# Attention merge: the third output tile's first nine products move ahead of the last division

## The chip, the core and the metric

The kernel runs on one core of one Trainium2 chip. The metric is the device time of one execution in microseconds (us), first instruction to last and the little that lies around them. Five engines work side by side, each in the order of its own instruction stream: TensorE (PE) multiplies matrices, VectorE (DVE) and ScalarE (ACT) work element by element, GpSimd (POOL) does small work, and SyncE (SP) starts most transfers. Products land in PSUM, which has eight banks; everything else is in SBUF.

## The reference, cut to what matters

One layer of a transformer trunk: two token mixers on the same input, merged by gates, then a feed-forward block.

```
mla_l = _blocked_attend(q_l, k_all, v_all).reshape(B, L, -1) @ w_mla_o
y_l = (jax.nn.sigmoid(gr_l) * ret_l + jax.nn.sigmoid(gm_l) * mla_l) @ w_out
```

There are 512 latent and 256 context tokens, eight attention heads of 64 values each and 1024 model features. The change touches the product with `w_mla_o` in the first line, and the merge by the gates in the second.

## The kernel before

**Numbers in two parts.** Every matrix product is made of three: each operand is split into a rounded part and the rest (`split`, L104: ACT casts the high part, L105, DVE subtracts for the low part, L106), and `mm3` (L119) multiplies high by high (L121), high by low (L122) and low by high (L123). A weight is loaded on SP's queue into one of three raw buffers (`wr`, L109) and split into one of three pair buffers (`w`, L115).

**The heads.** Heads 0 to 7 run one after the other. `mix(h)` (L624) makes six score tiles `st` by 128 keys, exponentiates them on ACT (`ex`, L642), splits them (`pt`) and multiplies them with the values into `po` (L654 to L656). Row 64 of `po` is the softmax sum: ACT copies it to `sums` (L658) and the rest to `ou` (L659). Between these stand pieces of the next heads: `row_max(h + 1)` (products `sc`, L612, a maximum on DVE, L614, a transpose `mr` and a copy into the query, L620), `queries(h + 2)` (`mq`, L597 to L602) and `keys` (`kn`, `knc`, `kl`, `kc`).

**The division.** Two heads make a pair, whose `ou` is divided by its sums and split into `om`. The first three pairs do it through DRAM (`reciprocals`, L681: `sums` is written out, read back spread over the partitions as `sm`, inverted by DVE, L687, written as `recd`, L688, and read back broadcast as `rb`, L691; `divided`, L694, multiplies by it, L695). The last pair does it in place with TensorE (`divide`, L661): four transposes into PSUM tile `s1` (L664), the reciprocal (L666), four transposes into `s2` (L670), a split `rr`, two products that spread it over the partitions into `s3` (L674, L675), the multiplication (L676) and the split into `om`.

**The merge.** `merge_mm(n, ks)` (L800) makes output tile `n` of 128 features in PSUM tile `mo`, from those of the four pairs that `ks` names, three products for each pair. One weight tile, of `w_mo[n // 2]`, serves two output tiles. Nine products of tile 0 stand inside the last head, nine of tile 1 behind it, then the division, and then the rest of the 96. Each finished tile is multiplied with one gate, added to the other branch and split into `mg` (L821 to L823), which the output projection `wo` reads.

**What sets the order.** The program names the order in which steps are asked for; a scheduler then places every instruction on its engine and gives each tile the buffer that comes free, so a step that moves can change the order of others far ahead of it. PSUM tiles `st`, `mq`, `kn`, `mr`, `mo`, `s1`, `s2` and `s3` share four banks (`pss`, L78). `sc` and `po` share four more (`psb`, L77).

Of the kernel before, what the change touches and what calls it, by code (L numbers as in the profile page):

```python
# [63 lines left out]
def block(ctx: ExitStack, tc: tile.TileContext, xc, xtok, crow, wada, bada, w_rg, w_rv, w_rqk, w_kv, w_dq,  # L64
# [27 lines left out]
    def half(shape, dt=F32, n="hp"):  # L92
        return hpp.tile(shape, dt, tag="hp", name=nm(n))
# [4 lines left out]
    def bank(n="ps"):  # L98
        return pss.tile([P, 512], F32, tag="ps", name=nm(n))
# [4 lines left out]
    def split(h, l, src):  # L104
        S.copy(h, src)  # L105
        V.tensor_tensor(l, src, h.bitcast(F32), ALU.subtract)  # L106
# [6 lines left out]
    def weight(ap, n=1024):  # L113
        r = load(ap, n)
        w = whl.tile([P, 2, 1024], F32R, tag="w", name=nm("w"))  # L115
        split(w[:, 0, :n], w[:, 1, :n], r[:, :n])
        return w

    def mm3(o, st, mv, start, stop, more=False):  # L119

        T.matmul(o, st[0], mv[0], start=start, stop=False, skip_group_check=more)  # L121
        T.matmul(o, st[0], mv[1], start=False, stop=False, skip_group_check=more)  # L122
        T.matmul(o, st[1], mv[0], start=False, stop=stop, skip_group_check=more)  # L123
# [161 lines left out]
    def feat(w, base=0, step=P, ktn=KT):  # L285
        def st(k):
            c = slice(base + k * step, base + k * step + P)
            return w[:, 0, c], w[:, 1, c]
        return st
# [235 lines left out]
    def run(g):  # L525
        for _ in g:
            pass
# [272 lines left out]
    def merge_mm(n, ks):  # L800
        if n % 2 == 0 and wm[n] is None:
            wm[n] = wm[n + 1] = weight(w_mo[n // 2])
        if mp[n] is None:
            mp[n] = bank("mo")
        st = feat(wm[n], (n % 2) * 512)
        for k in ks:
            mm3(mp[n], st(k), (om[k][:, 0], om[k][:, 1]), k == 0, k == 3)
# [3 lines left out]
        next(m)  # L811
    merge_mm(0, range(3))
    run(m)
    merge_mm(1, range(3))
    next(eg)
    om.append(divide(ou))
    mg = [eight([P, 2, NL], F32R, "mg") for _ in range(8)]
    for n in range(8):
        merge_mm(n, range(3, 4) if n < 2 else range(4))
        m = half([P, NL], n="mt")  # L820
        V.tensor_tensor(m, mp[n], gm[n // 2][:, n % 2], ALU.mult)  # L821
        V.tensor_tensor(m, m, gr[n // 2][:, n % 2], ALU.add)
        split(mg[n][:, 0], mg[n][:, 1], m)  # L823
# [513 lines left out]
```

## Time and profile before

| what | value |
|---|---|
| median of three runs | 975.82 us (974.88 to 976.2) |
| the profiled execution | 976.76 us |
| its span, first to last instruction | 975.0 us |
| around the span | 1.76 us |
| TensorE busy | 948.1 us of the span |
| mean granted TensorE clock | 0.995 |

The profile is of one execution, 0.94 us longer than the median of the runs. A row of the timeline has a start (us from the span's start), a duration, the engine, the source line, the operation, what it writes and reads, and in brackets how long the engine had been idle and what released it.

### The profile page before, as it was taken

The numbers are of one execution on the slowest core, as the hardware profiler recorded it, in microseconds if no ns is written. First come the engines' busy times: TensorE is split into PE (matmuls) and PEld (weight loads), VectorE is DVE, ScalarE is ACT, GpSimd is POOL, SyncE is SP. The second block draws the span as 40 slices with busy tenths as digits, with TensorE's granted clock in tenths as the row PEclk, the third lists the DMA queues.
The fourth block names the chain that finished last, engine by engine and source line by source line (L and its number), as shares of the span: only waits on it lengthen the run. The fifth ranks groups of instructions, "written<-read, shape, count | busy, mean of one in ns | idle before, by whom it ended". The sixth has DMA issues, their size and how long they took to land.

```text
span 975.0 us, 13864 instructions
## 1 busy us (share of the span) xinstructions
PE 948.1 (97%) x5354; PEld 806.8 (83%) x5354; DVE 703.1 (72%) x1117; ACT 451.4 (46%) x684; POOL 67.4 (7%) x91
## 2 busy tenths in 40 slices
PE   5999999999999999999998999999999999999996
PEld 3888888888899878877675777999999999988885
DVE  6949977676773554488887778697777666794957
ACT  3354263335233633257677455265555455653340
POOL 0000100100001101000000001122122110000100
PEclk9999999999999999999999999999999999999999
DMA  9845621441115369221002368579777762676671
GB/s 354 336 141 197 240 92 45 171 152 49 30 61 175 128 157 202 87 65 44 13 12 55 108 208 251 179 193 218 189 202 176 188 155 66 219 250 188 207 235 67
DMA packets 54734, 148.84 MB, mean 153 GB/s; under 512 B 9862, under 2 KB 11014, under 8 KB 54668
## 3 DMA queue, kind: packets, MB, share of 16 engines
q1 hardware_dynamic: 41580, 123.94, 39.2%
q0 software_dynamic: 6112, 11.54, 7.1%
q10 hardware_dynamic: 6976, 12.48, 4.1%
q8 instruction: 42, 0.69, 0.3%
q14 instruction: 24, 0.20, 0.1%
HBM read 142.13 MB, written 4.23 MB: 150 GB/s over the span
## 4 chain that ended last, share of the span: by engine, by line
PE 83%; DVE 7%; ACT 4%; issue 2%; DMA 2%; POOL 1%; DVEq 0%; SPq 0%; ACTq 0%; POOLq 0%
PE wd L122 4%; PE wd L123 4%; PE wd L121 4%; PE gy L121 3%; PE gt L121 3%; PE gt L123 3%; PE gt L122 3%; PE gy L122 3%; PE gy L123 3%; PE rva L123 2%; PE rva L121 2%; PE ro L123 2%; PE ro L122 2%; PE ro L121 2%; PE rva L122 2%
## 5 line engine op out<-in xcount | busy, mean ns | idle before, releaser
L105 ACT CAST w<-wr 128x1024 fp32r<-128x1024 f32 (+2 forms) x137 | 141.3, 1032 | 193.7 <-PE wd L123 47.6
L106 DVE TENSOR_TENSOR w<-wr,w 128x1024 fp32r<-128x1024 f32 (+2 forms) x137 | 164.3, 1200 | 70.7 <-ACT w L105 69.2
L121 PE MATMUL wd<-w,tt 128*128 128x512 f32 (+1 forms) x163 | 61.2, 375 | 0.0
L122 PE MATMUL wd<-w,tt 128*128 128x512 f32 (+1 forms) x163 | 60.9, 374 | 0.1
L123 PE MATMUL wd<-w,tt 128*128 128x512 f32 (+1 forms) x163 | 60.7, 373 | 0.0
L121 PE MATMUL gt<-hL,w 128*128 128x512 f32 x128 | 50.9, 398 | 0.2 <-DVE ck L483 0.2
L123 PE MATMUL gt<-hL,w 128*128 128x512 f32 x128 | 50.7, 396 | 0.0
L122 PE MATMUL gt<-hL,w 128*128 128x512 f32 x128 | 50.7, 396 | 0.0
L405 POOL TENSOR_TENSOR sm<-sm,mhalf 128x1 f32<-128x1 f32 x18 | 15.1, 840 | 452.2 <-DVE sm L404 452.1
L122 PEld LDWEIGHTS wd<-w,tt 128*128 128x128 f32 x163 | 30.6, 188 | 6.3 <-DVE w L106 0.4
L123 PEld LDWEIGHTS wd<-w,tt 128*128 128x128 f32 x163 | 30.7, 188 | 6.1
L121 PEld LDWEIGHTS wd<-w,tt 128*128 128x128 f32 x163 | 30.6, 188 | 5.8
L106 DVE TENSOR_TENSOR pt<-ex,pt 128x512 fp32r<-128x512 f32 x48 | 30.7, 685 | 6.1 <-ACT pt L105 5.9
L510 ACT ACTIVATE gate<-gt 128x512 f32<-128x512 f32 x16 | 9.6, 598 | 50.1 <-PE gt L123 50.1
L614 DVE TENSOR_REDUCE sm<-sc 128x1 f32<-128x768 f32 x32 | 29.6, 950 | 0.8 <-PE sc L613 0.6
L121 PEld LDWEIGHTS gt<-hL,w 128*128 128x128 f32 x128 | 24.1, 188 | 6.0 <-DVE ck L483 0.5
L123 PEld LDWEIGHTS gt<-hL,w 128*128 128x128 f32 x128 | 24.1, 188 | 5.8
L122 PEld LDWEIGHTS gt<-hL,w 128*128 128x128 f32 x128 | 24.1, 188 | 5.5
L105 ACT CAST w<-s 128x1024 fp32r<-128x1024 f32 x19 | 20.0, 1050 | 18.6 <-PE gx L123 18.6
L642 ACT ACTIVATE ex<-st 128x512 f32<-128x512 f32 x48 | 26.8, 596 | 3.6 <-PE st L123 3.5
L105 ACT CAST ap<-af 128x512 fp32r<-128x512 f32 x24 | 14.8, 621 | 27.3 <-DVE af L372 25.7
L106 DVE TENSOR_TENSOR w<-s,w 128x1024 fp32r<-128x1024 f32 x19 | 23.3, 1225 | 5.6 <-ACT w L105 5.4
(441 smaller groups left out, 3100.6 us busy)
## 6 DMA issues: line engine op xcount, KB each, us to landing
wr<-in_w_dn_dram SPq DMA_DIRECT2D x44, 512.0 KB, 4.3
wr<-in_w_gu_dram SPq DMA_DIRECT2D x25, 512.0 KB, 4.2
ada_m<-in_wada_dram SPq DMA_DIRECT2D x22, 512.0 KB, 5.3
s<-in_w_gu_dram SPq DMA_DIRECT2D x38, 256.0 KB, 4.6
s<-in_w_gu_dram POOLq DMA_DIRECT2D x38, 256.0 KB, 6.6
wr<-in_w_out_dram SPq DMA_DIRECT2D x16, 512.0 KB, 4.4
wr<-in_wada_dram SPq DMA_DIRECT2D x10, 512.0 KB, 3.7
wgb<-in_w_gu_dram SPq DMA_DIRECT2D x19, 256.0 KB, 4.7
```

Of the source, the lines that this page charges most:

```text
L105: S.copy(h, src)
L106: V.tensor_tensor(l, src, h.bitcast(F32), ALU.subtract)
L121: T.matmul(o, st[0], mv[0], start=start, stop=False, skip_group_check=more)
L122: T.matmul(o, st[0], mv[1], start=False, stop=False, skip_group_check=more)
L123: T.matmul(o, st[1], mv[0], start=False, stop=stop, skip_group_check=more)
L405: G.tensor_tensor(dst, dst, mhalf[:, :n], ALU.pow)
L510: S.activation(dst[n // 2][:, n % 2], ps, AF.Sigmoid)
L614: V.tensor_reduce(mx[:, t:t + 1], ps.rearrange("p a b -> p (a b)")[:, :NA], AX.X, ALU.max)
L642: S.activation(ex, ps, AF.Exp, scale=SSC)
```

## The change

Nine of the twelve products of output tile 2 (the three pairs that are divided already) are asked for ahead of the division, as those of tile 1 are; behind it, tile 2 has three products left instead of twelve. The number of products is the same.

```diff
     merge_mm(0, range(3))
     run(m)
-    merge_mm(1, range(3))
+    for n in range(1, 3):
+        merge_mm(n, range(3))
     next(eg)
     om.append(divide(ou))
     mg = [eight([P, 2, NL], F32R, "mg") for _ in range(8)]
     for n in range(8):
-        merge_mm(n, range(3, 4) if n < 2 else range(4))
+        merge_mm(n, range(3, 4) if n < 3 else range(4))
```

`next(eg)` loads and splits one weight of the feed-forward block (`in_w_gu_dram`, `wgh` and `wgl`). With the change the weight of tiles 2 and 3 (`w_mo[1]`) is asked for ahead of it.

TensorE's order at the last division, before the change. The tiles `mo794`, `mo795`, `mo817` are output tiles 0, 1 and 2, `om804` is the last pair's quotient, and the brackets name the engines that an instruction waits for:

```order
L670 MATMUL s2801_4656<-ident_92,sm800_4654 2x128 [waits DVE_49]
L670 MATMUL s2801_4656<-ident_92,sm800_4654 2x128 x3
L674 MATMUL s3803_4664<-rr802_4661,sel_3364 128x512 [waits Activation_49]
L675 MATMUL s3803_4664<-rr802_4661,sel_3364 128x512 [waits DVE_49]
L121 MATMUL mo817_4700<-om645_4016,w816_4697 128x512 [waits PE_49]
L122 MATMUL mo817_4700<-om645_4016,w816_4697 128x512
L123 MATMUL mo817_4700<-om645_4016,w816_4697 128x512
L121 MATMUL mo817_4700<-om710_4288,w816_4697 128x512
L122 MATMUL mo817_4700<-om710_4288,w816_4697 128x512
L123 MATMUL mo817_4700<-om710_4288,w816_4697 128x512
L121 MATMUL mo817_4700<-om770_4521,w816_4697 128x512
L121 MATMUL mo794_4615<-om804_4668,w793_4612 128x512 [waits Activation_49]
```

The same place with the change, where `mo798` is output tile 2, `mo819` tile 3 and `om807` the last pair's quotient:

```order
L123 MATMUL mo798_4648<-om770_4521,w797_4645 128x512
L664 MATMUL s1802_4664<-ident_92,sums505_3362 128x64 [waits Activation_49,Pool_49]
L664 MATMUL s1802_4664<-ident_92,sums505_3362 128x64 x3
L670 MATMUL s2804_4671<-ident_92,sm803_4669 2x128 [waits DVE_49]
L670 MATMUL s2804_4671<-ident_92,sm803_4669 2x128 x3
L674 MATMUL s3806_4679<-rr805_4676,sel_3364 128x512 [waits DVE_49]
L675 MATMUL s3806_4679<-rr805_4676,sel_3364 128x512
L121 MATMUL mo819_4718<-om645_4016,w797_4645 128x512 [waits DVE_49]
L122 MATMUL mo819_4718<-om645_4016,w797_4645 128x512
L123 MATMUL mo819_4718<-om645_4016,w797_4645 128x512
L121 MATMUL mo794_4615<-om807_4683,w793_4612 128x512 [waits Activation_49]
L121 MATMUL mo795_4633<-om807_4683,w793_4612 128x512
```

The nine products of tile 2 have moved from behind the division to ahead of it; three of tile 3 stand where they stood. With three `mo` tiles held, `s1`, `s2`, `s3` and tile 3 take the one bank that is left in turn (bank 6; before, `s1` and `s3` had bank 5, `s2` and tile 2 bank 6), so L674 now waits for DVE instead of ACT, and the first product behind the division waits for DVE.

VectorE's order at the start of head 4, some 50 us ahead of the division, as a difference. `w_4645` is `w_mo[1]`, `mq_4128` and `qf_4123` are the query of head 5, `sm_4158` its row maxima, and L687 is the reciprocal of the second pair:

```order
 L597 TENSOR_TENSOR qf_4123<-mq_4113,qtab_3344 128x512
 L599 TENSOR_TENSOR q_4125<-mq_4113,qtabs_3346 32x512
+L106 TENSOR_TENSOR w_4645<-wr_4643,w_4645 128x1024
 L600 TENSOR_TENSOR qf_4123<-qf_4123,q_4125 32x512
 L106 TENSOR_TENSOR mq_4128<-qf_4123,mq_4128 128x512
 L614 TENSOR_REDUCE sm_4158<-sc_4159 128x1
 L614 TENSOR_REDUCE sm_4158<-sc_4163 128x1
+L687 RECIPROCAL sm_4150<-sm_4150 128x8
 L614 TENSOR_REDUCE sm_4158<-sc_4167 128x1
-L687 RECIPROCAL sm_4150<-sm_4150 128x8
 L614 TENSOR_REDUCE sm_4158<-sc_4171 128x1
```

The split of `w_mo[1]` has come here from a place just ahead of the division (its cast on ACT likewise, to the last place before L620 of head 4). Later in the same head the division of the second pair, L695, has moved from behind L599 of head 6's query to a place three tiles earlier, and TensorE's `sc`, `po` and `mq` products of heads 4 to 6 stand in other orders, with none added.

SP's order of transfers at the same place, as a difference; `sumd`, `sm`, `recd` and `rb` are the second pair's way through DRAM:

```order
 L691 DMA rb_3882<-recd 64x512 x2
 L684 DMA sumd<-sums_3362 1x512 x2
+L110 DMA wr_4658<-in_w_gu_dram 128x1024
 L686 DMA sm_4150<-sumd 128x2x4
 L688 DMA recd<-sm_4150 128x2x4
```

A load of 512 KB that stood ahead of the first pair's way (where `w_mo[1]` is loaded now) stands inside the second pair's.

## Rows read from the trace of the kernel before

**Rows 1.** The page: busy time of each engine, share of the span, instructions

```profile
PE 948.1 (97%) x5354; PEld 806.8 (83%) x5354; DVE 703.1 (72%) x1117; ACT 451.4 (46%) x684; POOL 67.4 (7%) x91
```

**Rows 2.** Waits of TensorE from 400 to 570 us (total, times, longest)

```profile
PE st L121 <- ACT ex L642: 1.8, 1, 1.8
```

**Rows 3.** Timeline of all engines around the last division

```profile
540.31 0.40 PE L656 MATMUL po<-pt,mv 128*65 128x512 f32 x1
...
540.74 0.58 ACT L658 COPY sums<-po 1x512 f32<-1x512 f32 x1 [1.22 <-PE po L656]
...
542.40 0.39 PE L123 MATMUL mo<-om,w 128*128 128x512 f32 x1
...
542.73 0.46 PE L664 MATMUL s<-ident,sums 64*128 64x64 f32 x4
...
544.75 0.49 PE L674 MATMUL s<-rr,sel 2*128 2x512 f32 x1 [0.66 <-ACT rr L105]
...
545.46 0.69 PE L675 MATMUL s<-rr,sel 2*128 2x512 f32 x1 [0.22 <-DVE rr L106]
...
546.08 0.80 PE L121 MATMUL mo<-om,w 128*128 128x512 f32 x1
546.19 0.69 DVE L676 TENSOR_TENSOR ou<-s,ou 128x512 f32<-128x512 f32 x1 [0.78 <-PE s L675]
...
546.67 0.63 PE L122 MATMUL mo<-om,w 128*128 128x512 f32 x1
...
546.97 0.62 ACT L105 CAST om<-ou 128x512 fp32r<-128x512 f32 x1 [2.27 <-DVE ou L676]
...
547.62 0.69 DVE L106 TENSOR_TENSOR om<-ou,om 128x512 fp32r<-128x512 f32 x1 [0.74 <-ACT om L105]
...
548.38 0.63 PE L123 MATMUL mo<-om,w 128*128 128x512 f32 x1
```

**Rows 4.** Windows: stretch, length, busy times, granted clock (PEclk), DMA share, GB/s

```profile
531.20:535.40 4.20, 4.18 (x11) 2.69 (x12) 2.51 (x4) 4.20 (x9) 0.00 (x0) 0.59 0.41 125
546.10:549.50 3.40, 3.40 (x10) 2.75 (x10) 1.39 (x2) 0.62 (x1) 0.00 (x0) 0.57 0.41 135
```

**Rows 5.** The page's groups: the low parts of weights on VectorE

```profile
L106 DVE TENSOR_TENSOR w<-wr,w 128x1024 fp32r<-128x1024 f32 (+2 forms) x137 | 164.3, 1200 | 70.7 <-ACT w L105 69.2
```

**Rows 6.** Timeline of all engines, start of head 4

```profile
486.05 0.58 ACT L620 ACTIVATE mq<-mr 1x512 fp32r<-1x512 f32 x1 [3.67 <-PE mr L618]
...
486.66 0.68 DVE L600 TENSOR_TENSOR qf<-qf,q 32x512 f32<-32x512 f32 x1
...
487.26 0.24 SPq L684 DMA_DIRECT2D sumd<-sums  x1
...
488.36 0.61 ACT L105 CAST mq<-qf 128x512 fp32r<-128x512 f32 x1
...
488.44 0.38 SPq L686 DMA_DIRECT2D sm<-sumd  x1
...
489.02 0.50 PE L612 MATMUL sc<-kl,mq 128*128 128x512 f32 x1
...
489.73 2.69 DVE L614 TENSOR_REDUCE sm<-sc 128x1 f32<-128x768 f32 x3
...
495.34 1.56 SPq L691 DMA_DIRECT2D rb<-recd  x2
```

**Rows 7.** Timeline of SyncE's queue, the first pair's way through DRAM

```profile
458.45 0.35 SPq L110 DMA_DIRECT2D wr<-in_w_gu_dram  x1
459.01 0.24 SPq L684 DMA_DIRECT2D sumd<-sums  x1
462.26 0.38 SPq L686 DMA_DIRECT2D sm<-sumd  x1
```

**Rows 8.** Timeline of VectorE, the second pair's division

```profile
502.67 0.69 DVE L695 TENSOR_TENSOR ou<-ou,rb 128x512 f32<-128x512 f32 x1
```

**Rows 9.** The view of tile `rb`: its reads' time to landing

```profile
DMA to landing us min/median/max: 2.8/3.6/3.6
```

## The prediction

> **What bounds the kernel now.** I read the page first: TensorE is busy for 948.1 of the span's 975.0 us [rows 1], so nearly every microsecond in which it waits longer or shorter comes out at the end, and no other engine is near its limit. The list of its waits has 1.8 us once, for ACT's exponentials at the end of head 6 [rows 2], and little else around the change. The timeline of the division [rows 3] is the place to look closely. The last `po` product starts at 540.31; ACT has copied the sums by 540.74 + 0.58 = 541.32. TensorE comes to the transposes L664 only at 542.73, because nine products of tile 1 stand ahead of them: from 540.31 to 542.40 nine steps of 0.232 us each. So the division doesn't wait for the sums; it waits for TensorE's own queue, by 1.4 us. After L664 come 3.35 us, to 546.08, in which TensorE has transposes and two short products and nothing else. From 546.08 it works again, on tile 2, while L676 (546.19), the cast (546.97 + 0.62 = 547.59) and the low part (547.62 + 0.69 = 548.31) finish the quotient `om`. Those 2.2 us between 546.08 and 548.31 cost nothing today, since tile 2's products lie beside them.
>
> The windows view adds one thing: TensorE's granted clock is 0.57 of full speed in 546.10 to 549.50, and 0.59 in 531.20 to 535.40 [rows 4], both times just after it had little to do. At the lower level (1.2 GHz) a product takes (548.38 - 546.67) / 4 = 0.428 us [rows 3] against 0.232 at 2.4 GHz.
>
> **The change part by part.** *The nine products of tile 2 ahead of the division.* They run at 0.232 us each, so L664 starts 2.1 us later. TensorE is busy for all of it, so this costs nothing by itself; but it fills a gap that wasn't there (the sums were ready), and takes the cover from one that was.
>
> *The division itself.* In the order shown L674 waits for DVE instead of ACT, since `s3` lies in the bank of `s2` and must wait until both parts of `rr` are read. Today that read is over at 545.46, where L675 starts, 2.73 after L664 [rows 3]. So L674 starts at 2.73 instead of 2.02, and L675 one product later, 0.23 or 0.43 by the clock: 2.96 to 3.16. From L675's start to L676's start are 0.73, and L676 takes 0.69, so its end lies 4.38 to 4.58 after L664. Tile 3's first product waits for that, as it gets the same bank: some 0.07 later, 4.5. Today the first product behind the division starts at 3.35. TensorE loses **1.15 us** here. After that nothing more is lost: the high part of `om` comes 0.78 to 1.4 us after L676's end by the same rows, and three products of tile 3, then three high ones of tiles 0 to 2, cover that at either clock (0.7 and 1.4 us at full speed).
>
> The Trainium skill (Perfetto Trace Analysis, Optimization Strategy) reads gaps on the engine that should be saturated as a sign that SBUF or PSUM may be too small for the next tile. No row of the division before has that cause. By that rule the bank that is short would be the reason of the whole loss, and giving `s3` a bank of its own would give back the 0.71 at L674 and most of the wait for L676.
>
> *The end of the merge.* DVE then gets three finished tiles at once and, in its order, splits the second `w_out` weight only after tile 7's multiplication. Counted from TensorE's first `wo` product that is about 3.3 us (a multiplication and two additions of 0.6 to 0.7, a split of 1.2 [rows 3, 5]), and the second weight's low part is wanted after 12 products and one, 3.0 us. I put down **0.15** (bounds 0 and 0.4).
>
> *The split of `w_mo[1]` in head 4.* On ACT it is free: 3.67 us idle ahead of L620 [rows 6]. On DVE 1.2 us [rows 5] now stand ahead of L600, so head 5's query is ready at 488.5 instead of 487.34; its cast, behind one more exponential in ACT's order, starts near 489.6 instead of 488.36 [rows 6]. The score products follow at 490.3, where TensorE's new order has them after two more `st` tiles, so they don't wait; but the third waits for the first maximum: low part of the query 0.7, maximum 2.69 / 3 = 0.9, so 491.85, and TensorE is through with the second near 491.0. That is **0.85 us** of idle time where there was 0.1 or less. What else moves in head 4 I cost at nothing, since other products stand ready.
>
> *The load inside the second pair's way.* SP issues the 512 KB once that split is done, about 487.95, ahead of L686. Without a load ahead L686 follows L684 after 488.44 - 487.26 = 1.18 us [rows 6]; with one 0.56 us ahead, in the first pair, after 462.26 - 459.01 = 3.25 [rows 7]. So a small transfer lands about 2.1 us later behind a load. If the read of `sm` takes as long as that write, it is there near 488.44 + 3.3 = 491.7. L687 stands behind the second maximum in the new order, at 491.85 + 0.9 = 492.75, so the read is in time, but L687 comes 0.3 later than today (behind the third, 489.73 + 2.69 = 492.42 [rows 6]). The two `rb` reads (today 495.34, and the second 1.0 later [rows 6]) move by as much and need up to 3.6 us to land [rows 9]: 496.65 + 3.6 = 500.3. L695, which today runs at 502.67 without a wait [rows 8], now stands where DVE arrives near 499.4. DVE waits almost 1 us, head 6's query is that much later, and its first score product, placed three products earlier, finds it missing: **0.65 us**. The third pair's reciprocal is also later (behind the last maximum), which delays the last `pt` of head 6 and a `po` product: **0.5**. Against this the row maxima of heads 5 and 6 stand earlier, which gives back part of the waits ahead of the next heads: **-0.5**. Together heads 4 to 6: 0.85 + 0.65 + 0.5 - 0.5 = **1.5 us**; bounds 0 (all hidden) and 2.5 (nothing given back, and 0.5 more for reads that land late).
>
> *The clock.* I assume that the two slow stretches stay as they are. One costs (0.428 - 0.232) for each of its seven or so products, 1.4 us; it can go, or a further one can come.
>
> **The sum.** 1.15 + 0.15 + 1.5 = 2.8 us. On the profiled execution that is 976.76 + 2.8 = 979.6; that one lies 0.94 above the median of the runs, so in their terms 975.82 + 2.8 = **978.6 us**, slower by 0.29%. A measurement of this kernel can tell about 0.2%, 1.95 us, from no change: 977.77 is the border.
>
> **The rivals.** *The heads hide their part, and only the division costs* (not slower in what can be measured). For it: the 1.5 is laid out from places in an order and not from rows of such waits, and TensorE has other products around each of them. Against it: TensorE works through its stream in order, and a product that waits holds those behind it. Then 975.82 + 1.3 = 977.1; it decides from the point where heads 4 to 6 cost under 0.65. Chance 0.22.
>
> *One slow stretch fewer.* The stall of 1.8 us ahead of 531.2 and the division both shift; if the clock isn't lowered after one of them, 1.4 comes back. With the heads at nothing: 977.1 - 1.4 = 975.7, no change; 0.10. With both stretches gone 974.3, or less by what the runs scatter; I give 0.05 to faster.
>
> *One slow stretch more.* TensorE idles about 1.2 us longer inside the division and works on slowly behind it, and it has new idle time in heads 4 to 6. A further stretch adds 1.4: 980.0; 0.13. By the Trainium skill (TensorE: Matmul & The Clock Gate, HAM oscillation) gaps between bursts of products lower the clock again and again; the rows agree in so far as both lowered stretches follow gaps [rows 2 to 4].
>
> **How the numbers follow.** The forecast, both parts at work, has 0.50 and a range of its own of 977.8 to 979.8. Slower by over 0.2%: 0.50 + 0.13 = 0.63. Within 0.2%: 0.22 + 0.10 = 0.32. Faster: 0.05. The range leaves out the cases of fewer slow stretches (0.15) below, and some 0.04 above: 976.2 to 980.8.
>
> **What would show it.** In the profile after: L674 released by DVE; from L664 to the first `mo` product behind it 4.5 us instead of 3.35; that product released by DVE L676; a new wait of `sc` for L614 in head 4, and DVE waiting at L695 for `rb`. The start of head 7's scores would show the 1.5, the first `wo` product the whole. It is wrong if products hide the heads' waits, if L674 starts as early as before, or if the clock's stretches are other in number.

## The result: 985.63 us, slower by 0.9%, more than three times the forecast loss

| what | before | after |
|---|---|---|
| median of four runs each | 975.46 us | 985.63 us (982.74 to 986.28) |
| ratio, 95% interval | | 1.0093 [1.0076, 1.0111] |
| profiled execution / its span | 976.76 / 975.0 us | 986.28 / 984.5 us |
| mean granted clock | 0.995 | 0.993 |

The sign was right and the size was not: 978.6 was forecast, 980.8 was the upper end. TensorE has as many instructions as before [rows 1] and waits longer; its busy time is 3.2 us longer too, part of it at the lower clock (below):

```profile
PE 951.3 (97%) x5354; PEld 808.2 (82%) x5354; DVE 703.0 (71%) x1117; ACT 452.1 (46%) x684; POOL 67.5 (7%) x91
```

Its waits from 400 to 600 us after the change (total, times, longest); the first row is the one of before [rows 2]:

```profile
PE st L121 <- ACT ex L642: 1.8, 1, 1.8
PE s L674 <- DVE rr L106: 1.4, 1, 1.4
PE po L656 <- DVE pt L106: 1.2, 1, 1.2
PE wo L122 <- DVE w L106: 1.1, 2, 0.5
PE wo L121 <- ACT w L105: 0.9, 2, 0.8
PE st L121 <- ACT mq L620: 0.9, 2, 0.7
PE mo L121 <- DVE ou L676: 0.8, 1, 0.8
PE sc L612 <- DVE sm L614: 0.8, 1, 0.8
```

The second and seventh rows are the division that the prediction described; the third and eighth are the heads. The fourth and fifth are in a place where it expected 0.15 us: the output projection (`wo`), more than 30 us behind the division. The list counts four of them, 2.0 us. By the steps from one `wo` product to the next there are five (0.57, 0.92, 1.15, 0.93 and 0.52 us between 585.0 and 594.4, where 0.23 is usual), 2.9 us more than usual.

The division, in the timeline of all engines after (answers to [rows 3]):

```profile
544.48 0.40 PE L656 MATMUL po<-pt,mv 128*65 128x512 f32 x1
...
549.00 0.46 PE L664 MATMUL s<-ident,sums 64*128 64x64 f32 x4
...
551.74 0.49 PE L674 MATMUL s<-rr,sel 2*128 2x512 f32 x1 [1.38 <-DVE rr L106]
...
552.50 0.69 DVE L676 TENSOR_TENSOR ou<-s,ou 128x512 f32<-128x512 f32 x1 [0.82 <-PE s L675]
...
553.25 0.51 PE L121 MATMUL mo<-om,w 128*128 128x512 f32 x1 [0.78 <-DVE ou L676]
```

L674 waits for DVE, and from L664 to the first product behind it are 553.25 - 549.00 = 4.25 us where 4.5 was forecast and 3.35 stood before. But L676 starts 552.50 - 549.00 = 3.50 after L664, and before 546.19 - 542.73 = 3.46 [rows 3]: for VectorE, on whose result everything behind waits, the division isn't longer. It is later, since L664 starts 4.52 us behind the last `po` instead of 2.42.

What that does, together with VectorE's new order, is seen on SyncE's queue. Loads in the output projection, before and after (a load goes out when one of the three raw buffers `wr` is free):

```profile
560.13 0.33 SPq L110 DMA_DIRECT2D wr<-in_w_out_dram  x1
563.02 0.33 SPq L110 DMA_DIRECT2D wr<-in_w_gu_dram  x1
568.24 0.33 SPq L110 DMA_DIRECT2D wr<-in_w_out_dram  x1
571.03 0.33 SPq L110 DMA_DIRECT2D wr<-in_w_gu_dram  x1
572.77 0.33 SPq L110 DMA_DIRECT2D wr<-in_w_out_dram  x1
```

```profile
569.31 0.33 SPq L110 DMA_DIRECT2D wr<-in_w_out_dram  x1
574.30 0.33 SPq L110 DMA_DIRECT2D wr<-in_w_gu_dram  x1
576.64 0.33 SPq L110 DMA_DIRECT2D wr<-in_w_out_dram  x1
577.73 0.33 SPq L110 DMA_DIRECT2D wr<-in_w_gu_dram  x1
580.08 0.33 SPq L110 DMA_DIRECT2D wr<-in_w_out_dram  x1
```

The same loads, of `w_out[3]`, a `w_gu`, `w_out[4]`, a `w_gu` and `w_out[5]`, go out 9.2, 11.3, 8.4, 6.7 and 7.3 us later, while the first `wo` product is only 571.00 - 565.66 = 5.34 us later. Each goes out just when VectorE is through with the low part of the third weight before it. Those low parts of `w_out[0]` to `w_out[3]` began before at 558.84, 561.77, 566.99 and 569.78; after (timeline of VectorE):

```profile
568.02 1.22 DVE L106 TENSOR_TENSOR w<-wr,w 128x1024 fp32r<-128x1024 f32 x1
...
573.01 1.22 DVE L106 TENSOR_TENSOR w<-wr,w 128x1024 fp32r<-128x1024 f32 x1
...
575.35 2.35 DVE L106 TENSOR_TENSOR w<-wr,w 128x1024 fp32r<-128x1024 f32 x2
```

568.02 + 1.22 = 569.24, and the load of `w_out[3]` goes out at 569.31; 573.01 + 1.22 = 574.23, and the `w_gu` load at 574.30.

**Where the 9.5 us between the two profiled executions lie.** From the starts of the same products in both timelines: 0.6 at the last `po` of head 3 (486.08 to 486.69), ahead of everything that the change moves; 3.6 from there to the last `po` of head 7 (54.23 to 57.79), of which 1.1 is a longer stretch at the lower clock (below); 1.2 from there to the first `wo` (25.35 to 26.52); 3.2 from the first to the 97th `wo`, the first half of the projection (22.92 to 26.09); 1.0 from there to the end, which no run here follows up.

### The profile page after: what moved, and what is told of

Same layout as the page of the kernel before. It is cut to its first block, busy times and chain, and to the rows that moved or that the text cites. A ratio compares the mean times of both kernels' runs of the same rounds, so it can differ in the third digit from the quotient of the medians.

```text
span 984.5 us, 13862 instructions
## 1 busy us (share of the span) xinstructions
PE 951.3 (97%) x5354; PEld 808.2 (82%) x5354; DVE 703.0 (71%) x1117; ACT 452.1 (46%) x684; POOL 67.5 (7%) x91
## 4 chain that ended last, share of the span: by engine, by line
PE 83%; DVE 6%; ACT 4%; DMA 4%; issue 2%; POOL 1%; SPq 0%; DVEq 0%; ACTq 0%; POOLq 0%
PE wd L122 4%; PE wd L123 4%; PE wd L121 4%; PE gy L121 3%; PE gy L122 3%; PE gy L123 3%; PE gt L121 3%; PE gt L123 3%; PE gt L122 3%; PE rva L121 2%; PE rva L123 2%; PE ro L123 2%; PE ro L121 2%; PE ro L122 2%; PE rva L122 2%
## 5 line engine op out<-in xcount | busy, mean ns | idle before, releaser
L105 ACT CAST pt<-ex 128x512 fp32r<-128x512 f32 x48 | 27.3, 623 | 0.2
```

## The experiments

Runs of one kernel differ by up to 6.4 us, in part with the number and length of TensorE's stretches at the lower clock (the mean granted clock of single runs lies between 0.992 and 0.999), so each time is given with its interval beside the kernel before on the same chip. In most runs the order of some instructions is *held*: an edge between each and the next sets the order in which an engine's queue takes them, and no more.

```
for a, b in zip(ins, ins[1:]):
    tc.add_manual_dep(b.ins, a.ins.name, info, reason="row")   # info: NoSync
```

The table counts, in the timeline of TensorE of each profiled execution, us from the last `po` of head 7 to the first, the 97th and the last of the 192 `wo` products (*late clock*: whether the stretch behind the division ran partly at half the clock, which costs 1.5 to 2.7 ahead of the first `wo`).

| run | first `wo` | 97th | first to 97th | last | late clock | ratio [95%] |
|---|---|---|---|---|---|---|
| before | 25.35 | 48.27 | 22.92 | 73.14 | yes | |
| after | 26.52 | 52.61 | 26.09 | 77.64 | yes | 1.0093 [1.0076, 1.0111] |
| e1 hoist only | 25.40 | 48.22 | 22.82 | 73.48 | yes | 1.0035 [1.0019, 1.0051] |
| e2 products only | 26.50 | 52.47 | 25.97 | 78.79 | yes | 1.0050 [1.0031, 1.0069] |
| e3 + VectorE held | 26.51 | 53.88 | 27.37 | 78.09 | yes | 1.0048 [1.0030, 1.0065] |
| e4 order only | 23.85 | 48.88 | 25.03 | 73.96 | no | 1.0032 [1.0017, 1.0046] |
| e5 + ScalarE held | 26.47 | 51.53 | 25.06 | 75.75 | yes | 1.0042 [1.0028, 1.0057] |
| e6 change, both held | 26.53 | 51.22 | 24.69 | 75.43 | yes | 1.0086 [1.0063, 1.0109] |
| e7 division first | 23.83 | 46.36 | 22.53 | 74.49 | no | 1.0039 [1.0025, 1.0054] |
| e8 `s3` own bank | 23.84 | 49.25 | 25.41 | 74.04 | no | 1.0031 [1.0018, 1.0043] |
| e9 own buffers | 27.58 | 49.97 | 22.39 | 73.91 | yes | 0.9997 [0.9985, 1.0010] |
| e10 before, own buffers | 23.85 | 46.24 | 22.39 | 70.18 | no | 0.9984 [0.9973, 0.9995] |
| e11 change, own buffers | 27.72 | 50.12 | 22.40 | 74.04 | yes | 1.0044 [1.0029, 1.0059] |
| e12 division earlier, own buffers | 22.74 | 45.13 | 22.39 | 70.75 | no | 0.9962 [0.9947, 0.9977] |
| e13 hoist, third pair | 25.43 | 50.30 | 24.87 | 74.46 | yes | 1.0016 [1.0002, 1.0029] |
| e14 division earlier | 22.71 | 46.57 | 23.86 | 73.33 | no | 0.9995 [0.9981, 1.0008] |

**The first four: which part costs what.** e1 asks for the weight early and moves no product; e2 moves the products without asking earlier:

```diff
 e1, in the kernel before            e2, in the kernel after
+    wm[2] = wm[3] = weight(w_mo[1])  -    for n in range(1, 3):
     next(eg)                         -        merge_mm(n, range(3))
     om.append(divide(ou))            +    merge_mm(1, range(3))
                                           next(eg)
                                      +    merge_mm(2, range(3))
```

In e1 heads 4 to 6 and SyncE's order are those of the changed kernel, and VectorE's order in the merge that of before; in e2 it is the reverse. e3 is e2 with VectorE's merge held in the order of before; e4 is the kernel before with it held in the order of after (its casts on ScalarE then fall as in the changed kernel too).

> The kernel before, with the weights w_mo[1] asked for ahead of the next(eg) but the nine products of tile 2 left behind the division. Heads 4 to 6 and SyncE's transfers then stand in the order of the changed kernel, the merge behind the division in that of the kernel before. If the 9.8 us fall into three parts that add up (heads 4 to 6 about 2.5 to 3.3 with the longer slow stretch behind them, division about 1, output projection about 3), this one costs 2.5 to 3.5 us: 978 to 979.5. If instead the early load of w_mo[1] is what makes the loads of w_out late, the waits of the output projection are here too: 981 to 983.

> The change with the next(eg) ahead of tile 2's products instead of behind them: nine products in front of the division, heads 4 to 6 and SyncE's order as in the kernel before, VectorE's order in the merge as in the changed kernel. If the parts add up: division 1 and output projection 3, 979 to 981, with first waits of wo for w in the output projection. If the late loads come from the heads: 976.5 to 977.5, and no such waits.

> As the run with the products alone, and VectorE's instructions in the merge held in the order of the kernel before (m0 m1 a0 a1 m2 g0 g1 a2 m3, w_mo[3], g2 a3 m4, w_out[0], g3 a4 m5, w_out[1], ...) by edges that only set an order; TensorE's order then differs from the kernel before by the nine products alone. If VectorE's order is the cause of the late loads, only the division is left: about 1 us, 976.5 to 977.5, without waits of wo for w. If the moved products themselves make the loads late (the merge begins later but ends as fast), the time stays at 979 to 981.

> The kernel before with nothing changed but VectorE's order in the merge, which is held in that of the changed kernel (m4 m5 g3 a4 a5, w_out[0], g4 g5 m6 m7 a6 a7, w_out[1], g6 g7, w_out[2], w_out[3]); TensorE's and SyncE's orders are those of the kernel before. If VectorE's order makes the loads of w_out and w_gu late, this alone costs 2.5 to 3.5 us: 978 to 979.5, with waits of wo for w from the sixth w_out on, and the first w_gu load issued 8 us or more later than before. If the order costs only what it delays directly (as the prediction had it, 0 to 0.4): 975.5 to 976.5.

Measured: e1 979.94, e2 982.88, e3 980.92, e4 978.80 us, beside 975.70. Heads and merge nearly add up (0.35% and 0.50% for 0.93% together), and the late loads are not the heads' doing: e1 has one wait of `wo` of 0.5 us, e2 has 2.4 us of them. VectorE's order alone (with the casts that follow it) costs 0.32%, as its theory said. But that order is not the whole cause: e3 should have come down to 977 and did not. Its trace had a fault of its own. Holding VectorE alone let ScalarE's cast of `w_out[2]` slip ahead of a cast of the merge, and the cast waited for TensorE (timelines of ScalarE, then VectorE, of e3):

```profile
564.89 1.05 ACT L105 CAST w<-wr 128x1024 fp32r<-128x1024 f32 x1 [3.24 <-PE mo L127]
```

```profile
566.49 0.69 DVE L106 TENSOR_TENSOR mg<-mt,mg 128x512 fp32r<-128x512 f32 x1 [1.96 <-ACT mg L105]
```

So e3 decides nothing, and e5 repeats it with both engines held.

**The products alone, cleanly.** My theory then was that VectorE itself binds: from the division on it has no free time, so a division that starts 2.1 us later makes everything behind it 2.1 later.

> As the third run, but ScalarE's casts in the merge are held in the order of the kernel before as well (w_mo[3], g0 g1, w_out[0], g2 g3, w_out[1], g4 g5, w_out[2], g6, w_out[3], g7); in the third run a cast of w_out[2] that waits for TensorE had slipped ahead of g5 and held VectorE for 2 us. Now the nine products of tile 2 are the one difference to the kernel before. Theory of the chain: from the division on VectorE has no free time (multiplications, low parts, the splits that free the buffers of the loads), and the output projection waits for what it frees; so the division's later start counts in full: 2.1 us, 978 to 978.5. Theory of TensorE's idle time: only the 1.15 us of the division count, 976.8 to 977.3. If the loss of the second and third runs was all in the order of ScalarE's casts: within 0.5 us of before.

> The changed kernel with VectorE's and ScalarE's instructions in the merge held in the order of the kernel before. What is left is heads 4 to 6 (3.5 by the first run) and the nine products: 979.5 to 981.5 by the theory of the chain (2.1 for the products), 980 or less by that of TensorE's idle time (1.15). The changed kernel's own order then costs the rest, 4 us or more; if it stays at 984 or above, the order costs nothing here.

> The mirror image of the change: the kernel before with the nine products of tile 1, which stand ahead of the division, put behind it, the second transposes' result s3 in a bank of its own, and both engines' orders in the merge held as before. L664 then starts about 1.3 us earlier, as soon as the sums are copied; TensorE idles 0.8 us there and saves 0.9 at L674 and L675, where products now stand. Theory of the chain: VectorE's work begins 1.3 us earlier and the loads with it, 974.2 to 975 (up to 1.3 faster). Theory of TensorE's idle time: no change, 975.5 to 976.2.

> As the run with the nine products and both orders held, with s3 in a bank of its own, so that L674 need not wait for VectorE's read and tile 3's products need not wait for L676. By the theory of TensorE's idle time, and by the rule that the bank is short, this gives back the 1.15 us of the division: 975.5 to 976.2, as before. By the theory of the chain it gives back next to nothing, since L675 waits for the low part of rr all the same and the chain through L676 starts no earlier: 977.5 to 978.5.

e7 puts tile 1's nine products behind the division; e7 and e8 take `s3` from the other PSUM pool:

```diff
 e7, in the kernel before               e7 and e8
-    merge_mm(1, range(3))              -        ps = bank("s3")
     next(eg)                           +        ps = big("s3")[:, 0]
     om.append(divide(ou))
+    merge_mm(1, range(3))
```

Measured: e5 979.71, e6 983.72, e7 979.36, e8 978.78 us, beside 975.73. e5 differs from the kernel before in the place of nine products and what follows from it at the division, and is 0.42% slower, 4.0 us, or 2.7 to 5.6 by the interval: more than the 1.15 of the division. Not all of that is waiting: the mean granted clock of its executions is 0.9942, of those before on the same chip 0.9966, and that shortfall over the span is an estimated 2.3 us, which leaves 1.7, little more than the division. In its profiled execution 1.1 is lost up to the first `wo` (25.35 to 26.47) and 2.1 between there and the 97th (22.92 to 25.06). The second part looks like the 2.1 us by which the nine products hold up L664, but the trace doesn't bear that out. The load of `w_out[3]` does go out 2.0 us later than before, counted from the last `po` (21.79 for 19.82), those of `w_out[6]` and `w_out[7]`, for which TensorE then waits, only 1.1 and 0.9 later, no more than TensorE itself; they land later (below). In e6 the order of after is undone and 0.86% of the 0.93% stays, with intervals that overlap widely. Its loads go out nearly as before too, counted from the first `wo`. So what the new order costs once the products are moved isn't told apart from nothing.

e8 gives `s3` its bank. TensorE's waits at L674 and for L676 fall from 1.4 and 0.8 to 0.7 and nothing, and the waits of `wo` that follow are as long as in e5 (25.41 against 25.06). The time is 0.9 us less with intervals that overlap, so it isn't shown that the 1.15 comes back. e7 doesn't answer its question: it is faster up to the 97th `wo` (46.36), and then loses 3.3 us because the scheduler also moved eight `wo` products of the second half behind the transposes `zt`, which wait 2.2 us for ScalarE.

**Is it the buffers?** In e9 to e12 the three `w_gu` weights that are loaded between the `w_out` loads get pages of their own, with the order of SyncE's loads held too, so that a `w_out` load waits for the split of the `w_out` three places back, and no longer for that of a `w_gu` or of the `w_out` two places back:

```diff
-        r = load(w_gu[n], 1024)
+        r = page([P, 1024], n="wrp")          # for n in (3, 4, 5)
+        nc.sync.dma_start(r, w_gu[n])
```

e12 also takes e8's bank for `s3` and asks for tile 1's products as `merge_mm(1, range(1))` ahead of the division and `merge_mm(1, range(1, 3))` behind it; the scheduler then moves two of the nine.

> The nine products alone, orders of VectorE, ScalarE and SyncE in the merge and the first half of the output projection held as in the kernel before, and the three w_gu weights that are loaded there read into pages of their own instead of the ring of three raw buffers that they share with w_out. Nothing else is undone: the division starts 2.1 us later as in the run before. If the output projection waits because the loads wait for a raw buffer that VectorE frees late, its waits (2.1 us between its 49th and 97th product) go, and 1.2 us of the division are left: 976.5 to 977.5, and from the last po to the 97th wo product 49.0 to 49.8 us instead of 51.5. If the transfers themselves are too slow, or VectorE's splits come too late in any case, nothing changes: 979 to 980 and 51 us or more.

> The kernel before with the same three pages, so that the buffers' worth without the change is known. TensorE has no wait for weights in its output projection before, so nothing is to be won there: 975.3 to 976.3 by either theory, 48.2 us from the last po to the 97th wo product. If it is faster by 1 us or more, the ring held back the kernel before too and the run before this one proves less.

> The changed kernel with the three pages and all orders of the merge held as in the kernel before: what is left are heads 4 to 6 (3.5) and the division (1.2). By the theory of the late loads 979.5 to 981; if the loads are late for another reason, 982.5 or more.

> A version that goes the other way: of tile 1's nine products two are moved from ahead of the division to behind its first transposes, s3 has a bank of its own, so that products of tile 2 fill TensorE's waits ahead of L674 and L675, and w_gu's three loads have their own pages; orders held as before. L664 starts 0.45 us earlier and TensorE saves 0.9 us of idle time in the division. If the stage is bound by TensorE once the loads have buffers: 974.6 to 975.2, with one slow stretch of the clock fewer 973.5. If the transfers or VectorE bind it: 975.5 to 976.

Measured: e9 976.54, e10 973.99, e11 979.85, e12 972.36 us, beside 975.65. e9 has the division as late as e5 and is 3.2 us faster; no `wo` waits in it, nor in the other three. Its loads (SyncE's queue of e9; the fifth and sixth `w_out` go out at 564.68 and 569.60, in e5 at 567.95 and 572.03):

```profile
562.29 0.33 SPq L766 DMA_DIRECT2D wrp<-in_w_gu_dram  x1
564.68 0.33 SPq L113 DMA_DIRECT2D wr<-in_w_out_dram  x1
565.18 0.33 SPq L766 DMA_DIRECT2D wrp<-in_w_gu_dram  x1
569.60 0.33 SPq L113 DMA_DIRECT2D wr<-in_w_out_dram  x1
```

From the first to the 97th `wo` all four take 22.4 us; e5 took 25.06. So the later start of VectorE's work, which is still there in e9, costs nothing in that stretch, and VectorE alone doesn't bind: what binds is the three raw buffers that it frees. In e11, all of the change but its late loads, 0.44% is left (heads, division and clock), as expected. e10 came out better than expected, by 1.7 us, and its expectation says what that means: e9 proves less. The ring held back the kernel before as well, by 0.5 us in the first half of the projection of the profiled executions (22.92 to 22.39) and more in the second (24.87 to 23.94 from the 97th to the last). So of the 3.2 us that the pages give back in e9, 1.5 by the medians, or 2.8 by the ratios (0.45% in place of 0.16%), go with the moved products; the rest is won without them.

e12 beats both kernels: 0.9962 [0.9947, 0.9977], 3.3 us less than before by the medians. In its division TensorE has no wait that the list of waits shows, and the granted clock stays at 1.00 (windows view of e12, then its timeline from L664, which is line 669 there):

```profile
540.40:546.00 5.60, 5.60 (x26) 3.60 (x26) 2.18 (x5) 1.28 (x3) 0.00 (x0) 1.00 0.72 263
```

```profile
540.46 0.46 PE L669 MATMUL s<-ident,sums 64*128 64x64 f32 x4
...
542.54 0.40 PE L126 MATMUL mo<-om,w 128*128 128x512 f32 x1
542.87 0.50 PE L679 MATMUL s<-rr,sel 2*128 2x512 f32 x1
543.29 0.50 PE L127 MATMUL mo<-om,w 128*128 128x512 f32 x1
543.63 0.39 PE L128 MATMUL mo<-om,w 128*128 128x512 f32 x1
543.95 0.49 PE L680 MATMUL s<-rr,sel 2*128 2x512 f32 x1
```

**The last two** take the open points one at a time. e13 is e1 with the third pair's reciprocal L687 held ahead of the last row maximum, where it stands before; e14 is e12 without the pages.

> As the first run (w_mo[1] asked for early, products unmoved), with the third pair's reciprocal L687 held ahead of the fourth row maximum of the last head, where it stands in the kernel before; nothing else on VectorE, ScalarE or SyncE moves. If the third pair's late way through DRAM is what made heads 4 to 6 cost 2.5 to 3.5 us and not the 1.5 of the prediction, L687 comes 0.9 us earlier, L695 waits about 1 us less for rb, the wait of po for pt (1.3 us) falls to 0.2 to 0.5, and the time by about 1 us: 978.5 to 979.2 where the first run had 979.9. If that wait is made up elsewhere, or the excess sits in heads 4 and 5, the time stays within 0.4 us of the first run's.

> The version with the division 0.45 us earlier and products in TensorE's waits, with all orders held as before, but with w_gu's loads back in the ring of three raw buffers. Which of the two made that version 3.7 us faster? If TensorE binds the stretch in the kernel before, the division's 1.3 us (and a slow stretch of the clock) come back with or without the pages: 972.5 to 974. If the loads of w_out bind it, TensorE arrives earlier and waits for them, and only the 0.45 us by which VectorE starts earlier come back: 975 to 975.7, with waits of wo for w that the kernel before does not have.

Measured: e13 977.90, e14 976.39 us, beside 976.09. e13 gives back about half of what e1 lost (1.0035 to 1.0016, with intervals that overlap; the wait of `po` for the low part of `pt` is gone). The third pair in VectorE's timeline, after and then e13 (where the lines are two further):

```profile
522.90 0.19 DVE L687 RECIPROCAL sm<-sm 128x8 f32<-128x8 f32 x1
524.61 3.10 DVE L106 TENSOR_TENSOR pt<-ex,pt 128x512 fp32r<-128x512 f32 x5 [1.52 <-ACT pt L105]
529.66 0.69 DVE L695 TENSOR_TENSOR ou<-ou,rb 128x512 f32<-128x512 f32 x1 [1.96 <-DMA rb<-recd]
530.27 1.22 DVE L106 TENSOR_TENSOR wgl<-wr,wgh 128x1024 fp32r<-128x1024 f32 x1
531.40 0.68 DVE L106 TENSOR_TENSOR pt<-ex,pt 128x512 fp32r<-128x512 f32 x1
```

```profile
521.41 0.19 DVE L689 RECIPROCAL sm<-sm 128x8 f32<-128x8 f32 x1
...
527.16 0.69 DVE L697 TENSOR_TENSOR ou<-ou,rb 128x512 f32<-128x512 f32 x1
```

From the last `po` of head 3 to that of head 7, without a stretch at the lower clock in any of the three: e10 (heads as before) 52.67, e11 (heads as after) 55.15, e13 53.76 us. So heads 4 to 6 cost 2.5 us, and 1.4 of it is this one reciprocal.

e14 has the division of e12 and isn't told apart from the kernel before. TensorE comes to its first `wo` 2.6 us earlier than in the profiled execution of before (22.71; 1.5 of it are the clock), three of its `wo` products then wait 1.7 us in all for VectorE's low parts, and the last `wo` stands at 73.33 where it stood at 73.14. Without the pages nothing that could be measured was won in the division.

**When the loads go out, and when they land.** The first half of the projection ends with `w_out[7]`. The table follows its load in SyncE's and ScalarE's timelines: when it goes out, counted from the first `wo`, and how much later its cast starts, which waits for it to land.

| run | load goes out | to its cast | sum | first to 97th `wo` |
|---|---|---|---|---|
| before | 14.13 | 3.74 | 17.87 | 22.92 |
| e1 hoist only | 13.99 | 3.79 | 17.78 | 22.82 |
| e13 hoist, third pair | 14.25 | 5.60 | 19.84 | 24.87 |
| e5 products, orders held | 13.91 | 6.12 | 20.03 | 25.06 |
| e6 change, orders held | 14.41 | 5.25 | 19.66 | 24.69 |
| after | 15.82 | 5.22 | 21.04 | 26.09 |
| e14 division earlier | 14.75 | 4.04 | 18.79 | 23.86 |

In all seven, and in e3 and e8, the 97th `wo` stands 5.0 to 5.1 us behind that cast (5.2 to 5.6 in e7, e2 and e4; 8.2 with the pages). So this load sets the pace in the kernel before already, with no time to spare, and TensorE waits whether the load goes out later or lands later. In the profiled execution of after the 3.2 us are 1.7 of the one and 1.5 of the other; in e5 all 2.1 are the other. e13 shows that landing later needs no moved product. From the division on, its instructions stand in the order of e1, and this load goes out within 0.3 us of e1's, yet it lands 1.8 later, and the stretch is 2.0 longer (the load, then its cast, of e1 and then of e13):

```profile
583.85 0.33 SPq L110 DMA_DIRECT2D wr<-in_w_out_dram  x1
587.64 1.05 ACT L105 CAST w<-wr 128x1024 fp32r<-128x1024 f32 x1 [1.93 <-DMA wr<-in_w_out_dram]
```

```profile
579.64 0.33 SPq L110 DMA_DIRECT2D wr<-in_w_out_dram  x1
585.23 1.05 ACT L105 CAST w<-wr 128x1024 fp32r<-128x1024 f32 x1 [2.82 <-DMA wr<-in_w_out_dram]
```

What makes a load land late wasn't found. With the products moved and the ring in place the time to the cast is 5.2 to 6.2 us in all six traces, and without the move 3.7 to 4.4 in five of six, so the move may have a part in it; e13 says that it isn't the only reason.

## Why the prediction was wrong, step by step

**The step that failed** is the term "The end of the merge", 0.15 us with bounds 0 and 0.4, for which 3.2 us stand in the profiled execution. It looked at the second `w_out` weight, at the beginning of the projection, and asked when VectorE splits it, but not when the split frees a raw buffer, when the next load goes out, and when that lands. Nothing waits at the second weight; the waits come at the sixth to eighth, 15 us later, when the lead of the loads is used up. VectorE's new order alone (e4) costs 0.32% [0.17, 0.46], where the bounds allowed 0.04%. It sends the load of `w_out[5]` out 1.9 us later (9.02 us behind the first `wo`, for 7.11), and the first 97 products take 2.1 longer. In e6, which undoes that order, 1.8 of the 3.2 us stay, and with three buffers more none of it is left (e11, in the order of before; the new order with the pages was not run).

Under it lies the premise "TensorE is busy for all of it, so this costs nothing by itself". The nine products cost TensorE nothing, but L664 stands behind them in its queue, so the last `om` is finished 2.1 us later, and with it VectorE's merge begins later. The prediction took TensorE as the only bound because it was busy for 97% of the span [rows 1]. In the output projection of before it was busy because the loads came just in time: e14 shows that there was no slack, e9 to e12 that the raw buffers are the reason. That moving the products costs more than the 1.15 us is shown for the whole (e5, 0.42%); how much the later start of the merge has in it isn't, since an estimated 2.3 of e5's 4.0 us are the clock, and in its trace TensorE waits for loads that land late.

**The division, 1.15:** measured 0.90 from L664 to the first product behind it (4.25 for 3.35) and 1.17 to the first `wo`, by the steps described. The size was right. One reading was not: the high part of `om` is written 0.78 to 1.40 us after L676's start, not its end, on which no term hung. What TensorE gains there without the pages is lost again in waiting for loads (e14).

**Heads 4 to 6, 1.5 with bounds 0 and 2.5:** 2.5, at the bound. The wait of `sc` for the row maximum came (0.75 us for 0.85). The late second pair didn't: L695 waited 0.23 us for `rb`, where "almost 1 us" stood, and head 6's query was in time, so 0.65 was too much. The third pair was mis-sized: 0.5 put down, 1.4 by e13. L687 comes 0.9 us later behind the fourth maximum, `rb` lands after 2.8 to 4.4 us, and VectorE, which holds the low part of `pt` behind L695, waits 1.96 us.

**The clock, 0:** in the profiled execution two slow stretches, as assumed, but the first ran longer (windows view of after: the stretch behind the wait that ends at 534.34, and the one behind the division):

```profile
534.30:541.10 6.80, 6.76 (x18) 4.54 (x19) 4.20 (x7) 6.80 (x13) 0.00 (x0) 0.57 0.29 83
553.20:557.00 3.80, 3.75 (x10) 2.88 (x11) 1.00 (x2) 0.62 (x1) 0.00 (x0) 0.57 0.41 140
```

6.8 us at 0.57 where 4.2 stood at 0.59 [rows 4]. That is 1.1 us more. The profiled execution of before had more of the lower clock than most. Over all executions the mean granted clock is 0.9965 before (94 of them, beside e1 to e14) and 0.9940 after (4), and the shortfall over the span is an estimated 2.4 us, so the clock took more than any other term but the heads and the end of the merge. The two stretches of before bear the estimate out: by [rows 4] they make a shortfall of 1.7 and 1.5 us, and they cost 1.6 and 1.5 against executions without them (54.23 to 52.67 and 25.35 to 23.85).

**The rivals.** That the heads hide their part, or that a slow stretch goes, fell with the result. The rival with one slow stretch more had the direction of the clock's part and not the time. None of them names what cost most: a wait far behind the change, for loads that no term follows. The rule of the Trainium skill that the prediction weighed (Perfetto Trace Analysis, Optimization Strategy) says that a gap that comes back on the engine that should be busy can mean too little SBUF or PSUM for the next tile. I applied it to PSUM and to `s3`, where what e8 gave back isn't told apart from nothing. Its other half, SBUF, fits: the same wait of `wo` comes back in the changed kernel, and none is left with three more raw buffers there (e9, e11).

## What to carry to other kernels

That an engine is always busy doesn't make it free to move work ahead on it. Ask what stands behind the moved work in that queue, follow it through the other engines until a buffer comes free, and compare the time when the next load lands with the time when it is wanted, many microseconds further on. One profiled execution can mislead here: e1 and e13 have the same order from the division on and differ by 2.0 us in the projection. A ring of load buffers that two streams of weights share runs out of lead late: the place of the wait tells which stage starves, and SyncE's issue times beside the ends of the splits that free the buffers, and beside the casts that wait for the landing, tell why. With a scheduler between the program and the queues, hold the orders one engine at a time and then together, since holding one alone can let another slip (e3).

## What the runs showed of the hardware

The wait of 1.8 us for ScalarE at the end of head 6 is the same in all sixteen profiled executions. In or just behind it the granted clock fell to half in seven of them (before, after, e1, e2, e6, e7, e14) and stayed at 1.00 in nine. Where it fell it stayed down for 3 to 4 us in four executions and for 6 to 7 us in after, e1 and e6. In those three a wait of 1.2 to 1.3 us (`po` for `pt`) lies just ahead of the other; e11 has both waits too and its clock didn't fall. So the waits alone don't decide it, and what does wasn't found. Such a stretch costs 1.5 to 2.7 us, more than most terms of the sum, and is part of why runs of one kernel here lie up to 6.4 us apart.

A load of 512 KB in the first half of the projection (`w_out[7]`, table above) took from 3.7 to 6.2 us from its issue to the cast that waited for it, and by e1 and e13 this differs by 1.8 us between kernels whose instructions stand in the same order there.

The prediction's reading of the second such rule (the Trainium skill, TensorE: Matmul & The Clock Gate, HAM oscillation), that gaps between bursts of products lower the clock, agrees in so far as no stretch at half clock was seen behind a division without waits (e12, e14); but e4 and e10, whose division waits as before, had none either, so no run here shows that the waits are the reason.
